# Two layers of a hybrid decoder on one core: six of eleven FFN chunks as Strassen pairs, rows normalised before the transposes, rope's addition on VectorE

## The chip, the core and the metric

One core of one Trainium2 chip runs the whole kernel as one program. The metric is the device time of one execution in microseconds (us). Engine names are those of the profile: PE is TensorE's matmul, PEld its weight load, DVE is VectorE, ACT ScalarE, POOL GpSimd, SP the engine that issues the loads. PE reads its operands from SBUF and writes to PSUM, here eight banks of 128 x 512 floats.

## What is computed

The input is 256 tokens of 1024 floats. Two layers follow each other, and each adds two things to the tokens: a mixer of three attention groups and a SwiGLU FFN with 2816 hidden columns.

```python
h = rms_norm(x, attn_norm_g[l])
proj = h @ w_in[l]
...
mix = jnp.concatenate([merge_heads(moba), merge_heads(diff), merge_heads(dsa)], axis=-1)
x = x + mix @ w_out[l]

h2 = rms_norm(x, ffn_norm_g[l])
x = x + (jax.nn.silu(h2 @ w_gate[l]) * (h2 @ w_up[l])) @ w_down[l]
```

Queries and keys of the groups are normalised by head and turned by rope; the DSA group keeps the 64 best keys of each query by an indexer's scores.

## The kernel before

**Tiles.** The 256 tokens are two token tiles (t0, t1) of 128. The 1024 input columns are eight contraction tiles (kt) of 128, in two halves (hf): 0 to 3 and 4 to 7. The FFN's 2816 columns are eleven chunks (fc) of 256; a gate and an up chunk lie side by side, so one matmul gives 256 columns of gate and 256 of up in one bank.

**Three matmuls for one.** All large products are made from float32 values that are split into a high and a low part (`mm3`, L440 to L451): high times high, high times low, low times high. So a weight is loaded as 128 x 2048 floats into one of three `raw` buffers, its high part `wh` is written by ACT (`high_thread`, L403) and its low part `wl` = raw - wh by DVE (`low_thread`, L411; L418), each in two pieces of 1024 columns. Such a unit stands in one of four HL slots until PE has used it (`drop`). The normalised tokens are split in the same way into `hH` and `hL` (L486), the mixers' output into `mH` and `mL`, the FFN's hidden values into `dqk_f4`.

**One layer.** The projection into eight groups of columns (`project`, L1143), the mixers, the output projection with w_out (L1264 to L1284), the norm of the result (`norm`, L512), and the FFN: chunk by chunk gate and up, 2 token tiles x 8 kt x 3 = 48 matmuls of 512 columns, and one chunk later down, 24 matmuls (L1312 to L1350).

**The norm.** When a token tile's half is added to the tokens (`residual_thread`, L528), PE transposes it at once (L465), DVE multiplies by the gain (L481), ACT writes the high part and DVE the low part (L486). The row's factor `rx` is made beside that: ACT squares (L496), POOL adds, scales and raises to the power -1/2 (L508, L455, L458). It is used only behind the matmuls, in `glu_thread` (L1003, L1007) and by the mixers.

**Rope.** DVE multiplies the bank by two tables (L549, L552, L561), POOL adds the two products (L570), and POOL also makes each head's factor (L455, L458, L605, L611). Keys are then multiplied by it on DVE (L658) and transposed by PE.

**What sets the order.** Threads yield operations to a planner (`Timeline`, L73), which keeps a clock for each engine, takes the operation that can start first (by rank where they tie) and writes each engine's instructions down in that order. Copies may go to ACT or DVE. So every engine runs a fixed list and stops at an instruction whose inputs aren't there. SP issues the loads in the order of `plan`, each when its `raw` buffer is free.

Of the kernel before, what the change touches and what calls it, by code (L numbers as in the profile page):

```python
# [15 lines left out]
P = 128  # L16
# [32 lines left out]

OUT_ORDER = [(0, 1), (6, 7), (2, 3), (4, 5)]  # L50


class Slots:


    def __init__(self, tiles):
        self.free = [(0.0, n, t) for n, t in enumerate(tiles)]
        self.index = {id(t): n for n, t in enumerate(tiles)}

# [113 lines left out]
def hybrid_block(  # L173
# [105 lines left out]
    PT = slots(8, [P, 3 * P], "pT")  # L279
# [3 lines left out]
    mT = tuple(tile_([P, KT, S], F32R, tag=f"m{e}") for e in "HL")  # L283
    mH, mL = mT
    rc = tile_([P, NT, 6, HD], tag="rc")
    rs = tile_([P, NT, 6, HD], tag="rs")
    iqT = tile_([P, 4, S], tag="iqT")
    ikT = tile_([P, 1, S], tag="ikT")
    sqT, skT = tile_([P, 2, S], tag="sqT"), tile_([P, 2, S], tag="skT")
    mqT, mkT = sqT, skT  # L290
    sv, mv = [[tile_([P, 256], tag="v") for t in range(NT)] for _ in range(2)]
    dv = [tile_([P, 512], tag="dv") for t in range(NT)]
    sco = [tile_([P, S], tag="sco") for t in range(NT)]
# [63 lines left out]
    plan = []  # L357
    for l in range(depth):
        for name in CHUNKS:
            c0, c1 = CHUNKS[name]  # L360
            for kts in chunk_units(l, name):
                plan.append(((l, name, kts[0]), load_cols(w_in[l], kts, c0, c1)))
        for kts in OUT_ORDER:
            plan.append(((l, "out", kts[0]), load_cols(w_out[l], kts, 0, D)))
        for fc in range(NFC + 1):
            if fc < NFC:
                for kts in (lo4, hi4):
                    plan.append(((l, "gu", fc, kts[0]), load_gu(l, fc, kts)))
            if fc > 0:
                plan.append(  # L370
                    ((l, "down", fc - 1), load_cols(w_down[l], [2 * fc - 2, 2 * fc - 1], 0, D))
                )
    units = {
        key: {"n": n, "w": w, "dma": dma, "raw": Event(),
              "h": [Event() for _ in range(0, n, PIECE)],
              "ready": [Event() for _ in range(0, n, PIECE)]}
        for key, (n, w, dma) in plan
    }
    ahead = [0]

    def load_thread():
        for n, u in enumerate(units.values()):
# [12 lines left out]
            raw = yield ("get", RAW)  # L395
            u["tile"] = raw
# [6 lines left out]
    def high_thread():  # L403
        for u in units.values():
            yield ("wait", u["raw"])
            u["hl"] = yield ("get", HL)
            for n, cs in enumerate(pieces(u["n"])):
                t = yield copy_op(u["hl"][0][:, cs], u["tile"][:, cs], cs.stop - cs.start, True)
                u["h"][n].done(t)

    def low_thread():  # L411
        for u in units.values():
            for n, cs in enumerate(pieces(u["n"])):
                yield ("wait", u["h"][n])
                (h, lo), raw = u["hl"], u["tile"]
# [5 lines left out]
            RAW.put(raw, t)  # L421
            ahead[0] += 1

    def split_rank():
        return 5 if ahead[0] < 2 else 60

# [42 lines left out]
    def norm_thread(t, hf, g0, ready):  # L469

        yield ("wait", x_ready[t][hf])
        bank = yield ("get", BANK)
        b = quarters(bank)
        yield transposes(
            [(b[:, j, :], xt[t][:, (4 * hf + j) * P : (4 * hf + j + 1) * P]) for j in range(4)]
        )
        xg = yield ("get", W2)
# [4 lines left out]
        BANK.put(bank, e)  # L482
        ks = slice(4 * hf, 4 * hf + 4)
# [3 lines left out]
        W2.put(xg, e)  # L487
        ready.done(e)

    def square_thread(t, hf, first, both):  # L490
        yield ("wait", x_ready[t][hf])
        yield ("wait", first)
# [19 lines left out]
    def norm(g0):  # L512
# [3 lines left out]
        for t in range(NT):  # L516
            both = Event(2)
            for hf in range(2):
                tl.spawn(norm_thread(t, hf, g0, h_ready[t][hf]), 0)
                tl.spawn(square_thread(t, hf, h_ready[t][hf], both), 1)  # L520
# [14 lines left out]
    def rope_apply(bank, b, nh, cv, sv_, dst):  # L535
# [34 lines left out]
        e = yield G(150 + 2.2 * n, lambda: nc.gpsimd.tensor_add(dst, dst, bb))  # L570
# [58 lines left out]
    def qk_thread(t, bank, full, r_ready, parts, rstd, done, r_done):  # L629
# [9 lines left out]
        read = yield from rope_apply(bank, b, 8, rc[:, t, js], rs[:, t, js], q)  # L639
# [27 lines left out]
    def idx_thread(t, bank, full, r_ready, done):  # L667
# [22 lines left out]
        yield from to_pairs(q, [iqT[:, 1:4, :], ikT], t, own)  # L690
# [3 lines left out]
    def sv_iq_thread(t, bank, full, r_ready, done, v_done):  # L694
# [6 lines left out]
        e = yield copy_op(sv[t], bank[:, 0:256], 256, scale=rx[t], bank=bank)  # L701
# [3 lines left out]
        yield from to_pairs(q[:, 0:2, :], [iqT[:, 0:1, :]], t, own)  # L705
# [11 lines left out]
    def indexer(t, ready, done, rank):  # L717
# [3 lines left out]
        sc = sco[t][:, :n]  # L721
# [3 lines left out]
        for g in range(4 // per):  # L725
# [3 lines left out]
            def scores():  # L729
                for i in range(per):  # L730
                    for e in range(2):
                        rows = slice(HD * e, HD * e + HD)
                        nc.tensor.matmul(
                            two[e][:, i * n : (i + 1) * n], iqT[rows, g * per + i, toks(t)],
# [116 lines left out]
    def get_pTs(n):  # L851
        got = []
        for _ in range(n):
            got.append((yield ("get", PT)))
# [15 lines left out]
    def plain_out(t, pTs, se, v, kt0, ready, used, done):  # L870
# [11 lines left out]
        if used.count == 0:  # L882
            for pT in pTs.values():
                PT.put(pT, used.time)
# [13 lines left out]
        h, lo = mH[:, ks, toks(t)], mL[:, ks, toks(t)]  # L898
# [47 lines left out]
    def diff_out(l, t, aTs, ready, used, done):  # L946
# [37 lines left out]
        h, lo = mH[:, 2:6, toks(t)], mL[:, 2:6, toks(t)]  # L984
# [433 lines left out]
```

## Time and profile before

| | us |
|---|---|
| median of 3 runs | 668.76 (668.53 to 668.90) |
| the profiled execution | 668.79 |
| its span, first to last instruction | 667.0 |
| PE busy, DVE busy, ACT busy, POOL busy | 650.0, 440.0, 357.1, 116.4 |
| FFN of layer 0, from the last residual of its norm on | 150.5 to 336.0 |
| FFN of layer 1 | 482.5 to 663.4 |

The page gives each engine's busy time, the span in 40 slices, the chain of work that ended last, and groups of instructions by line with the mean time of one. In a row of the timeline stand the start, the time taken, the engine, the line, the operation, out<-in with shapes, and in brackets the idle time before it with what ended it. A duration reaches to the instruction's end; the next may start earlier, so the distance from start to start is the cost in a row of equal ones.

### The profile page before, as it was taken

The numbers are of one execution on the slowest core, as the hardware profiler recorded it, in microseconds if no ns is written. First come the engines' busy times: TensorE is split into PE (matmuls) and PEld (weight loads), VectorE is DVE, ScalarE is ACT, GpSimd is POOL, SyncE is SP. The second block draws the span as 40 slices with busy tenths as digits, with TensorE's granted clock in tenths as the row PEclk, the third lists the DMA queues.
The fourth block names the chain that finished last, engine by engine and source line by source line (L and its number), as shares of the span: only waits on it lengthen the run. The fifth ranks groups of instructions, "written<-read, shape, count | busy, mean of one in ns | idle before, by whom it ended". The sixth has DMA issues, their size and how long they took to land.

```text
span 667.0 us, 8918 instructions
## 1 busy us (share of the span) xinstructions
PE 650.0 (97%) x3252; PEld 535.7 (80%) x3252; DVE 440.0 (66%) x782; ACT 357.1 (54%) x668; POOL 116.4 (17%) x143
## 2 busy tenths in 40 slices
PE   8899999999999999999999998999999999999997
PEld 7776778887888888888888777788878888888886
DVE  5789999568555555555486999964855555555542
ACT  5566759547444444444356585876554444444430
POOL 1818460104100000000022466401000000000000
PEclk9999999999999999999999999999999999999999
DMA  8982333535655555555447036343375556656501
GB/s 245 324 270 63 128 127 129 188 122 170 214 190 190 189 190 189 189 187 167 151 144 252 20 108 223 103 162 106 123 234 189 190 189 190 190 189 190 189 1 63
DMA packets 73775, 111.28 MB, mean 167 GB/s; under 512 B 2658, under 2 KB 54660, under 8 KB 73732
## 3 DMA queue, kind: packets, MB, share of 16 engines
q1 hardware_dynamic: 73700, 110.71, 51.4%
q8 instruction: 25, 0.41, 0.3%
q14 instruction: 18, 0.15, 0.1%
q10 hardware_dynamic: 32, 0.01, 0.0%
HBM read 109.66 MB, written 1.05 MB: 166 GB/s over the span
## 4 chain that ended last, share of the span: by engine, by line
PE 77%; DVE 13%; POOL 6%; DMA 2%; issue 1%; ACT 1%; SPq 0%; POOLq 0%; ACTq 0%
PE bank L447 23%; PE bank L449 23%; PE bank L448 23%; PE bank L465 4%; DVE wl L418 3%; PE bank L866 2%; POOL qr L570 2%; DVE sco L766 1%; DVE sco L755 1%; POOL rs L1129 1%; POOL rq L458 1%; DVE small L765 1%; PE bank L816 1%; DVE qr L549 1%; DVE small L596 1%
## 5 line engine op out<-in xcount | busy, mean ns | idle before, releaser
L418 DVE TENSOR_TENSOR wl<-raw,wh 128x1024 fp32r<-128x1024 f32 (+4 forms) x209 | 252.9, 1227 | 60.7 <-ACT wh L234 57.2
L234 ACT ACTIVATE wh<-raw 128x1024 fp32r<-128x1024 f32 (+3 forms) x208 | 211.2, 1039 | 68.6 <-PE bank L449 54.6
L447 PE MATMUL bank<-wh,hH 128*128 128x512 f32 (+3 forms) x608 | 238.9, 393 | 0.3 <-ACT hH L234 0.3
L449 PE MATMUL bank<-wh,hL 128*128 128x512 f32 (+3 forms) x608 | 231.8, 381 | 0.8 <-DVE hL L486 0.8
L448 PE MATMUL bank<-wl,hH 128*128 128x512 f32 (+3 forms) x608 | 231.5, 381 | 0.0
L447 PEld LDWEIGHTS bank<-wh,hH 128*128 128x128 f32 x608 | 114.4, 188 | 23.0 <-issue 3.6
L449 PEld LDWEIGHTS bank<-wh,hL 128*128 128x128 f32 x608 | 114.2, 188 | 22.9 <-DVE hL L486 1.6
L448 PEld LDWEIGHTS bank<-wl,hH 128*128 128x128 f32 x608 | 114.5, 188 | 18.5
L1003 ACT ACTIVATE p<-bank,rx 128x256 f32<-128x256 f32 x44 | 20.9, 475 | 121.0 <-PE bank L449 121.0
L1007 DVE SCALAR_TENSOR_TENSOR p<-bank,rx,p 128x256 f32<-128x256 f32 x44 | 21.3, 484 | 90.2 <-ACT p L1003 90.2
L447 PE MATMUL bank<-wh,dqk_f 128*128 128x512 f32 x176 | 70.2, 399 | 0.0
L449 PE MATMUL bank<-wh,dqk_f 128*128 128x512 f32 x176 | 68.8, 391 | 0.0
L448 PE MATMUL bank<-wl,dqk_f 128*128 128x512 f32 x176 | 68.7, 390 | 0.0
L508 POOL TENSOR_TENSOR ss<-ss 128x1 f32<-128x1 f32 x8 | 2.6, 328 | 240.6 <-ACT w L496 240.6
L234 ACT ACTIVATE dqk_f<-bank 128x256 fp32r<-128x256 f32 (+1 forms) x52 | 21.6, 415 | 32.7 <-PE bank L465 32.6
L449 PEld LDWEIGHTS bank<-wh,dqk_f 128*128 128x128 f32 x176 | 33.0, 188 | 7.0
L448 PEld LDWEIGHTS bank<-wl,dqk_f 128*128 128x128 f32 x176 | 33.1, 188 | 6.4
L447 PEld LDWEIGHTS bank<-wh,dqk_f 128*128 128x128 f32 x176 | 33.1, 188 | 6.3
L570 POOL TENSOR_TENSOR qr<-qr,w 128x512 f32<-128x512 f32 (+2 forms) x24 | 32.5, 1356 | 28.3 <-DVE w L561 13.8
L1019 DVE TENSOR_TENSOR dqk_f<-bank,dqk_f 128x256 fp32r<-128x256 f32 x44 | 18.5, 421 | 23.0 <-ACT dqk_f L234 23.0
L465 PE MATMUL bank<-ident,qr 128*128 128x128 f32 x116 | 20.9, 283 | 9.9 <-DVE qr L658 5.9
L797 ACT ACTIVATE p<-p,small 128x128 f32<-128x128 f32 (+1 forms) x64 | 28.5, 448 | 3.2 <-DVE small L786 3.2
(111 smaller groups left out, 658.1 us busy)
## 6 DMA issues: line engine op xcount, KB each, us to landing
raw<-in_w_in_dram SPq DMA_DIRECT2D x22, 1024.0 KB, 5.1
raw<-in_w_gate_dram SPq DMA_DIRECT2D x44, 512.0 KB, 3.9
raw<-in_w_up_dram SPq DMA_DIRECT2D x44, 512.0 KB, 5.1
raw<-in_w_down_dram SPq DMA_DIRECT2D x22, 1024.0 KB, 5.0
raw<-in_w_out_dram SPq DMA_DIRECT2D x8, 1024.0 KB, 4.9
raw<-in_w_in_dram SPq DMA_DIRECT2D x4, 768.0 KB, 6.3
raw<-in_w_in_dram SPq DMA_DIRECT2D x2, 912.0 KB, 5.0
raw<-in_w_in_dram SPq DMA_DIRECT2D x3, 456.0 KB, 4.9
```

The costliest lines, as they stand in the source:

```text
L234: nc.scalar.activation(dst, src, AF.Copy)
L418: lambda: nc.vector.tensor_sub(lo[:, cs], raw[:, cs], h[:, cs].bitcast(F32)),
L447: nc.tensor.matmul(o, aH[:, kt, tok], wH[:, k, cols], start=start, stop=False)
L448: nc.tensor.matmul(o, aH[:, kt, tok], wL[:, k, cols], start=False, stop=False)
L449: nc.tensor.matmul(o, aL[:, kt, tok], wH[:, k, cols], start=False, stop=stop)
L465: nc.tensor.transpose(o, i, ident)
L570: e = yield G(150 + 2.2 * n, lambda: nc.gpsimd.tensor_add(dst, dst, bb))
L797: lambda: nc.scalar.activation(p[:, spans[t]], p[:, spans[t]], AF.Exp, bias=mn[:, t : t + 1], scale=-1.0, accum_out=se[t],),
L866: nc.tensor.matmul(o, pT[:, toks(t)], v[0][:, cols], start=True, stop=t == 0)
L1003: FC, lambda: nc.scalar.activation(ff, bank[:, 0:FC], AF.Silu, scale=rx[t]), ap=1, bank=bank
L1007: lambda: nc.vector.scalar_tensor_tensor(ff, bank[:, FC : 2 * FC], rx[t], ff, op0=OP.mult, op1=OP.mult),
L1019: e = yield V(256, lambda: nc.vector.tensor_sub(lo, b2[:, 0:2, :], h.bitcast(F32)), bank=bank2)
```

## The change

**Strassen pairs.** Of the eleven chunks, (2, 3), (5, 6) and (8, 9) are computed in pairs. The normalised tokens are a 2 x 2 block matrix A (token tile by contraction half), the weights of the two chunks a 2 x 2 block matrix B (contraction half by chunk). Plain, that is eight block products of 12 matmuls; the pair takes seven: P1 = A11 B11, P7 = S3 T3, Q5 = S1 T1, P6 = S2 T2, Q3 = S4 B22, P2 = A12 B21, Q4 = A22 T4. The token sums S1 to S4 are made once a layer (`a_sums_thread`) by four additions or subtractions on DVE, and split like the tokens. The weight sums T1 to T4 of each pair are made on DVE by `sums_thread` from unsplit weights, 2048 columns each, into the buffers of weights that are no longer needed, and are split like weights: seven units a pair for four. ACT copies P1 and Q5 out of PSUM, and DVE combines the products in seven operations of 512 columns (`strassen_thread`) before silu and multiplication. Between Q3 and P2 stands the down product of the chunk before.

**Buffers.** The extra weights need three more buffers E a layer. They are the mixers' buffers, which now share memory with them: the rope tables and scores (`tb`), and `mH` and `mL` once the output projection is over. The token sums lie where the probabilities and values were (`pv`), the kept tokens and hidden values where queries and keys were (`qk`).

**Rows normalised first.** Sums over token tiles need normalised rows, so the FFN's norm now waits for `rx`, multiplies the row by it, and only then transposes.

**First token tile.** The output projection goes (0, 1) of t0, (0) of t1, (2, 3) of t0, (1) of t1, (2, 3) of t1, where it went (0, 1) of t0 and t1, (2, 3) of t0 and t1.

**Rope.** The addition is DVE's.

```diff
+BLOCKS = [(0,), (1,), (2, 3), (4,), (5, 6), (7,), (8, 9), (10,)]
...
+        def third(i, j):
+            b12, b22, t3 = loads[l, "gu", j, 0], loads[l, "gu", j, 4], units[l, "T3", i]
...
+            e = yield from add(t3, b12["held"].tile, b22["held"].tile)
...
+            yield from add(t1, b11["held"].tile, b12["held"].tile)
+            e = yield from add(t2, t3["held"].tile, b11["held"].tile, units[l, "gu", i, 0])
+            t3["held"].used(e)
+            if after:
+                yield from third(*after)
+            yield ("wait", b21["raw"])
+            e = yield from add(t4, t2["held"].tile, b21["held"].tile, t2)
...
-    def norm_thread(t, hf, g0, ready):
+    def norm_thread(t, hf, g0, ready, r_ready, kept):
...
+        if r_ready:
+            yield ("wait", r_ready)
+            src = yield ("get", W2)
+            yield copy_op(src, xt[t][:, cs], 512, True, scale=rx[t])
...
+        sums = (
+            (w2, a21, a22, True), (a21, a11, a21, True), (a11, w2, a11, True), (a12, a12, a11, False)
+        )
...
-        e = yield G(150 + 2.2 * n, lambda: nc.gpsimd.tensor_add(dst, dst, bb))
+        e = yield add_op(dst, dst, bb, n)
...
+            for us, t in (((0, 1), 0), ((0,), 1), ((2, 3), 0), ((1,), 1), ((2, 3), 1)):
...
+                steps = [
+                    ("P1", (lo8, 0), (l, "gu", i, 0)),
+                    ("P7", s3, (l, "T3", i)),
+                    ("Q5", s1, (l, "T1", i)),
+                    ("P6", s2, (l, "T2", i)),
+                    ("Q3", n4, (l, "gu", j, 4)),
+                    None,
+                    ("P2", (hi8, 0), (l, "gu", i, 4)),
+                    ("Q4", (hi8, 1), (l, "T4", i)),
+                ]
```

How the lists of the engines change is shown at three places. Lines are those of each kernel; the numbers are buffers. First DVE at the start of layer 0's FFN. Before:

```order
L528 TENSOR_TENSOR x_1_71<-x_1_71,bank1_64 128x512
L418 TENSOR_TENSOR wl_25_100<-raw_17_92,wh_24_99 128x1024
L481 TENSOR_TENSOR w2_27_102<-bank3_66,gcol_6_80 128x512
L528 TENSOR_TENSOR x_1_71<-x_1_71,bank5_68 128x512
L418 TENSOR_TENSOR wl_25_100<-raw_17_92,wh_24_99 128x1024
L486 TENSOR_TENSOR hL_73_148<-w2_27_102,hH_72_147 128x4x128
```

Now, from the second half's residual of t0 on to the first silu product:

```order
L698 TENSOR_TENSOR x_1_71<-x_1_71,bank3_66 128x512
L248 TENSOR_SCALAR w2_27_102<-x_1_71,rx_69_144 128x512
L494 TENSOR_TENSOR wl_25_100<-raw_17_92,wh_24_99 128x1024
L612 TENSOR_TENSOR qk_91_1362<-bank7_70,gcol_6_80 128x512
L612 TENSOR_TENSOR qk_91_1362<-bank0_63,gcol_6_80 128x512
L698 TENSOR_TENSOR x_2_72<-x_2_72,bank2_65 128x512
L619 TENSOR_TENSOR hL_65_140<-qk_91_1362,hH_64_139 128x4x128 x2
L494 TENSOR_TENSOR wl_25_100<-raw_17_92,wh_24_99 128x1024
L698 TENSOR_TENSOR x_2_72<-x_2_72,bank4_67 128x512
L612 TENSOR_TENSOR qk_91_1362<-bank5_68,gcol_6_80 128x512
L503 TENSOR_TENSOR mL_93_1396<-tb_90_1343,mH_92_1395 128x1024
```

Before, a gain (L481) follows its residual at once; now both halves of t0 are added before the first gain (L612), a weight split stands ahead of the last residual, and the first weight sum (L503) inside the norm.

Second, DVE between a later pair's product P6 and its combinations, where before a chunk looked like this:

```order
L418 TENSOR_TENSOR wl_23_98<-raw_15_90,wh_22_97 128x1024 x2
L1007 SCALAR_TENSOR_TENSOR p_33_108<-bank0_63,rx_92_167,p_33_108 128x256
L1019 TENSOR_TENSOR dqk_f4_109_1407<-bank7_70,dqk_f4_109_1407 128x2x128
L418 TENSOR_TENSOR wl_25_100<-raw_16_91,wh_24_99 128x1024 x2
L1007 SCALAR_TENSOR_TENSOR p_38_113<-bank6_69,rx_93_168,p_38_113 128x256
```

```order
L1201 TENSOR_TENSOR w2_28_103<-bank0_63,w2_29_104 128x512
L503 TENSOR_TENSOR raw_17_92<-raw_17_92,raw_16_91 128x1024
L494 TENSOR_TENSOR wl_21_96<-raw_16_91,wh_20_95 128x1024
L503 TENSOR_TENSOR raw_17_92<-raw_17_92,raw_16_91 128x1024
L494 TENSOR_TENSOR wl_21_96<-raw_16_91,wh_20_95 128x1024
L503 TENSOR_TENSOR qr_31_106<-qr_30_105,w2_28_103 128x512
L494 TENSOR_TENSOR wl_23_98<-raw_17_92,wh_22_97 128x1024
L1201 TENSOR_TENSOR w2_28_103<-bank7_70,w2_28_103 128x512
```

The sum T4 (L503), the splits of P2's and Q4's weights (L494) and the combinations (L1201) alternate on one list, and the combination that waits for P6 stands first.

Third, SP's loads around the second pair. Before, and now:

```order
L338 DMA raw_16_91<-in_w_gate_dram 128x4x256
L338 DMA raw_16_91<-in_w_up_dram 128x4x256
L325 DMA raw_17_92<-in_w_down_dram 128x2x1024
L338 DMA raw_15_90<-in_w_gate_dram 128x4x256
L338 DMA raw_15_90<-in_w_up_dram 128x4x256
```

```order
L338 DMA raw_15_90<-in_w_down_dram 128x2x1024
L351 DMA raw_16_91<-in_w_gate_dram 128x4x256
L351 DMA raw_16_91<-in_w_up_dram 128x4x256
L351 DMA mH_92_1395<-in_w_gate_dram 128x4x256
L351 DMA mH_92_1395<-in_w_up_dram 128x4x256
L351 DMA mL_93_1396<-in_w_gate_dram 128x4x256
L351 DMA mL_93_1396<-in_w_up_dram 128x4x256
L351 DMA raw_15_90<-in_w_gate_dram 128x4x256
```

The loads of the next pair's second chunk into the extra buffers (mH, mL) stand ahead of the single chunk's first load (raw_15) on the one queue.

More of the change, by code (lines that the diff above doesn't have):

```diff
@@ L355, in chunk_units, with __init__, used, unit @@
         return [lo4, hi4]
-    plan = []
+    loads = {}
+    sequence = []
+    units = {}
+    class Held:
+        def __init__(self, uses):
+            self.uses, self.when, self.tile, self.slots = uses, 0.0, None, None
+        def used(self, when):
+            self.uses -= 1
+            self.when = max(self.when, when)
+            if self.uses == 0:
+                self.slots.put(self.tile, self.when)
+    def unit(key, n, w, held, raw):
+        count = len(range(0, n, PIECE))
+        units[key] = {
+            "n": n, "w": w, "held": held, "raw": raw if raw else [Event() for _ in range(count)],
+            "h": [Event() for _ in range(count)], "ready": [Event() for _ in range(count)],
+        }
@@ L361, in hybrid_block @@
             for kts in chunk_units(l, name):
-                plan.append(((l, name, kts[0]), load_cols(w_in[l], kts, c0, c1)))
+                load((l, name, kts[0]), load_cols(w_in[l], kts, c0, c1))
         for kts in OUT_ORDER:
[L364 to L378, printed above, removed]
+            load((l, "out", kts[0]), load_cols(w_out[l], kts, 0, D))
+        plan_ffn(l)
     ahead = [0]
     def load_thread():
-        for n, u in enumerate(units.values()):
+        for n, u in enumerate(loads[key] for key in sequence):
             if n in X_FIRST:
@@ L638, in qk_thread @@
         js = slice(parts[0][2], parts[-1][2] + 1, 3)
-        read = yield from rope_apply(bank, b, 8, rc[:, t, js], rs[:, t, js], q)
+        read = yield from rope_apply(bank, b, 8, cur["rc"][:, t, js], cur["rs"][:, t, js], q)
         yield ("wait", ev["read"])
@@ L1288, in main, with f4_of, get @@
+            for tag in ("mH", "mL"):
+                E[l].add(tile_([P, 2048], tag=tag, own=False), e)
+            f4s = []
+            def f4_of(fc):
+                def get():
+                    yield ("wait", kept["over"])
+                    if not f4s:
+                        f4s.append(tile_([P, 4, 4, S], F32R, tag="qk", own=False))
+                    return f4s[0][:, fc % 4]
+                return get
             fev = [[Event() for t in range(NT)] for fc in range(NFC)]
@@ L1352, in hybrid_block @@
+            yield from down_block(before)
     lam_ready = Event()
```

406 lines of the change are left out of this document (301 added, 105 removed).

## Prediction

> **What bounds the kernel now.** I read the page from its top: busy time, then the slices, then the chain that ended last.
>
> ```profile
> PE 650.0 (97%) x3252; PEld 535.7 (80%) x3252; DVE 440.0 (66%) x782; ACT 357.1 (54%) x668; POOL 116.4 (17%) x143
> PE   8899999999999999999999998999999999999997
> DVE  5789999568555555555486999964855555555542
> POOL 1818460104100000000022466401000000000000
> PEclk9999999999999999999999999999999999999999
> PE 77%; DVE 13%; POOL 6%; DMA 2%; issue 1%; ACT 1%; SPq 0%; POOLq 0%; ACTq 0%
> ```
>
> PE (TensorE) is busy for 97% of the span at full clock, and the chain runs over it for 77%. DVE (VectorE) has two faces: nines in both mixers (the 4th to 7th slice and the 23rd to 26th), fives in both FFNs. The windows give both stages in numbers:
>
> ```profile
> 16.70:100.00 83.30, 77.06 (x427) 62.43 (x428) 77.16 (x186) 52.79 (x112) 48.99 (x54) 1.00 0.55 182
> 150.50:336.00 185.50, 185.12 (x838) 151.78 (x837) 103.87 (x118) 87.79 (x119) 9.92 (x15) 1.00 0.57 183
> 482.50:663.40 180.90, 180.44 (x814) 147.54 (x812) 92.22 (x108) 77.75 (x105) 0.94 (x3) 1.00 0.51 166
> ```
>
> After the span, PE, PEld, DVE, ACT and POOL stand in that order. In the FFN of layer 0 (second row) PE works 185.1 of 185.5 us and DVE 103.9: only fewer matmuls can shorten this stage, and DVE has 81.6 us to give. In the first mixer DVE is busy for 77.16 of 83.3 us; there PE idles 6.2 us, and the waits name what for:
>
> ```profile
> PE bank L465 <- DVE qr L658: 5.9, 9, 1.0
> PE bank L465 <- POOL qr L570: 1.9, 3, 0.9
> PE bank L465 <- DVE qr L686: 1.5, 1, 1.5
> ```
>
> They are transposes that wait for the last step of a key, of an index row or of rope: 9.3 us over both layers.
>
> **Removed: 72 matmuls.** A Strassen pair takes 7 products of 12 matmuls where two plain chunks take 96 matmuls, so a pair saves 12, and six pairs 72.
>
> ```profile
> 240.08 0.39 PE L447 MATMUL bank<-wh,hH 128*128 128x512 f32 x1
> ...
> 240.76 0.39 PE L447 MATMUL bank<-wh,hH 128*128 128x512 f32 x1
> ...
> 336.82 1.91 PE L465 MATMUL bank<-ident,x 128*128 128x128 f32 x16
> ```
>
> The rows last 0.39 us because they overlap; what counts is start to start, (240.76 - 240.08) / 3 = 0.227 us. 72 x 0.227 = **-16.3 us**, all of it on the path, since PE never waits there. A transpose costs 1.91 / 16 = 0.12 us; their number stays the same.
>
> **Added: work on VectorE.** Its price is start to start too when it works without a pause:
>
> ```profile
> 451.62 2.36 DVE L418 TENSOR_TENSOR wl<-raw,wh 128x1024 fp32r<-128x1024 f32 x2 [2.22 <-ACT wh L234]
> 147.33 0.69 DVE L528 TENSOR_TENSOR x<-x,bank 128x512 f32<-128x512 f32 x1 [0.19 <-PE bank L449]
> 337.63 1.88 DVE L481 TENSOR_TENSOR w<-bank,gcol 128x512 f32<-128x512 f32 x3
> 445.92 0.42 DVE L889 TENSOR_TENSOR qr<-bank,se 128x256 f32<-128x256 f32 x1
> 446.26 0.17 DVE L886 RECIPROCAL se<-se 128x4 f32<-128x4 f32 x1
> 471.01 1.22 DVE L418 TENSOR_TENSOR wl<-raw,wh 128x1024 fp32r<-128x1024 f32 x1
> 478.03 1.22 DVE L418 TENSOR_TENSOR wl<-raw,wh 128x1024 fp32r<-128x1024 f32 x1
> ```
>
> One 1024-column operation lasts 1.22 us, two in a row 2.36, so the pitch is 1.14. By the same reading 512 columns cost 0.60 ((1.88 - 0.69) / 2, with 0.69 for one alone), and 256 cost 0.34 (446.26 - 445.92). A pair adds three weight units to split (6 x 1.14), four weight sums (8 x 1.14) and seven combinations of 512 columns: 16.0 + 4.2 = 20.2 us. Three pairs and the eight 512-column operations that form the token sums (4.8) make 65.4 us a layer: of the 81.6 us of slack, 81.6 - 65.4 - 8.2 = 8.0 are left in a stage that is 8.2 us shorter. DVE goes to some 95%.
>
> So the average fits, barely; what matters is each stretch, since only four split units (HL) can stand ready.
>
> *A later pair.* From one pair to the next PE does 204 matmuls (48 of a single chunk, 84 of a pair, 72 of three down products) and 12 transposes: 46.3 + 1.4 = 47.7 us. By the order, DVE does 32 operations of 1024 columns, 7 of 512 and 12 of 256 in it: 36.5 + 4.2 + 4.1 = 44.8 us, 94%. In its tightest part, from product P6 to the second weights of the next single chunk, I lay DVE's rows end to end (the first combination can start when P6 ends; 8.2 us later PE wants P2's weights, 10.9 later Q4's, 13.6 later the next chunk's): P2's are split after 0.6 + 4 x 1.14 = 5.2, Q4's after 8.7, the chunk's first after 12.2. Everything is ready 1.4 to 3 us early. I take 0.3 us of waiting for each of four such pairs, **+1** (0 to 4).
>
> *The first pair of a layer* has less lead, because the token sums and the first weight sums stand in front of it. From the second token tile of chunk 0 to the second weights of chunk 4, PE does 216 matmuls and 8 transposes, 49.9 us; DVE does 34, 14 and 7 operations, 38.8 + 8.4 + 2.4 = 49.6, and begins about 3.5 us later (its last split of the norm is wanted after 12 matmuls and two more, 3.2, and a 0.34 stands behind it). The last half unit is wanted 6 matmuls (1.4 us) later: 3.5 + 49.6 - 49.9 - 1.4 = 1.8 late. I take 1.5 for each layer, **+3** (0 to 9).
>
> [...]
>
> ACT gets the same six splits a pair and two copies:
>
> ```profile
> L234 ACT ACTIVATE wh<-raw 128x1024 fp32r<-128x1024 f32 x197 | 203.4, 1055 | 65.5 <-PE bank L449 54.6 <-DMA raw<-in_w_in_dram 7.1 <-issue 1.7
> L234 ACT ACTIVATE dqk_f<-bank 128x256 fp32r<-128x256 f32 x44 | 16.8, 382 | 24.2 <-PE bank L465 24.1
> ```
>
> 18 x 1.06 = 19 us and some 9 us of smaller copies on 87.8 of 185.5: hidden, at nothing, as long as its queue isn't blocked by a product that it waits for. Four transposed results and a chunk's result must share four free banks at a pair's end: one eviction (ACT 0.38, DVE 0.34) may show once a layer, **+1** (0 to 2).
>
> **Rows normalised first.** The transposes now wait for the row's factor, so POOL's steps stand between residual and matmul:
>
> ```profile
> 147.71 0.61 ACT L496 ACTIVATE w<-x 128x512 f32<-128x512 f32 x1
> 148.24 0.18 ACT L496 ACTIVATION_READ_ACCUMULATOR w<-x 128x1 f32 x1
> 148.50 0.19 POOL L508 TENSOR_TENSOR ss<-ss 128x1 f32<-128x1 f32 x1 [18.23 <-ACT w L496]
> 148.78 0.19 POOL L455 TENSOR_SCALAR rx<-ss 128x1 f32<-128x1 f32 x1
> 149.06 0.55 POOL L458 TENSOR_TENSOR rx<-rx,nhalf 128x1 f32<-128x1 f32 x1
> L591 ACT ACTIVATE w<-bank,rx 128x512 f32<-128x512 f32 x14 | 9.6, 687 | 10.2 <-PE bank L449 5.6 <-DVE w L552 1.7 <-issue 1.6
> ```
>
> Residual 0.69 (its row stands above), square and read 0.8, POOL 1.1 (148.50 to 149.61), scaling 0.69, transposes 0.5, gain 0.69, high part 0.6, low part 0.69: 5.8 us with hand-overs of about 0.1 each 6.4. For the first token tile the new order leaves 36 matmuls (8.2 us) behind it, where 24 (5.4) stood: covered. For the second, chunk 0 of the first tile covers 24 matmuls and 8 transposes, 6.4. In DVE's and ACT's queues a weight split (1.14, 1.06) stands ahead at one place each. I take 0.5 a layer, **+1** (0 to 6).
>
> **Rope's addition moves** from POOL to DVE, 24 times.
>
> ```profile
> L570 POOL TENSOR_TENSOR qr<-qr,w 128x512 f32<-128x512 f32 x16 | 22.5, 1405 | 15.0 <-DVE w L552 11.1 <-DVE w L561 3.9
> 22.52 2.28 DVE L418 TENSOR_TENSOR wl<-raw,wh 128x1024 fp32r<-128x1024 f32 x1
> 22.56 1.15 POOL L570 TENSOR_TENSOR qr<-qr,w 128x448 f32<-128x448 f32 x1
> ```
>
> 1.4 us and two hand-overs become 0.60 on an engine that is there already, and POOL's power steps no longer queue behind it. DVE gains some 6 us of work a layer where it is 93% busy, but such an addition can hold up a DVE operation beside it (2.28 instead of 1.22). Both ends: the 9.3 us of waits go but for a third (-6), or half of DVE's 12.5 us (16 x 0.60 and 8 shorter) shows on PE (+6). The keys' factor on POOL stays on the path, so I take a quarter of the waits, **-2.5**.
>
> Table building for layer 1 (POOL) now waits for the buffer tb; it has the last 120 matmuls (27 us) as cover: 0. The load bytes are the same.
>
> **Sum**, against the profiled execution's 668.79 us (span 667.0, 1.8 around it; the median 668.76 is the same): -16.3 + 1 + 3 + 1 + 1 - 2.5 = -12.8, so **656.0 us**.
>
> **Rivals.**
> *VectorE binds in the FFN (slower than before)*: if alternating sums, splits and combinations cost 1.22, 0.69 and 0.42 each, start to start, the first stretch takes 54.1 us of DVE, so it is 1.8 + 4.5 = 6.3 late, and a later period 49.0 where PE needs 47.7, with no room for a wait, some 2 late. 2 x 6.3 + 4 x 2 = 20.6 stand where the sum has 4: 672.5. It decides from a pitch of about 1.21 (47.7 of 44.8 times 1.14) on. For it: DVE at 95%, with no stage of this length to compare with. Against: the 2.36 for two, and the 1.88 for three. 7%. [...]
> *Loads starve the pairs (slower)*: SP issues in order, and a pair's two loads into the extra buffers now stand ahead of the next chunk's raw loads. If such a buffer comes free late, all behind it are late by a landing:
>
> ```profile
> raw<-in_w_gate_dram SPq DMA_DIRECT2D x44, 512.0 KB, 3.9
> raw<-in_w_up_dram SPq DMA_DIRECT2D x44, 512.0 KB, 5.1
> ```
>
> 5.1 us at each of six pairs is 31 us, less some 10 that the split units ready ahead give: 677. It decides where an extra buffer frees less than 5.1 us before the sum that reads it. In my laying-out it frees some 10 us before. 4%.
> *The mixers get longer*: DVE has 6.1 us free in the 83.3 of the first mixer's window and gets 6 more; if half of its 12.5 us over both layers shows on PE, +6 stands where the sum has -2.5: 664.5. 7%.
> *The waits go and DVE keeps ahead*: rope -6, and +2 where the sum has +6 for pairs, norms and banks: 648.5 to 651. 15%.
> *It doesn't do what it says*: PE's order holds 3014 rows' instructions for 3086, so the 72 are gone; 3% that something else takes up their time, 669.
>
> **Numbers.** The forecast's own band, 651 to 662, has 64%. The range, 649.5 to 664.5, takes in the rivals on the mixers and on the waits; the rest, 14%, is left out. A measurement of this kernel tells about 0.2% (1.3 us) from no change. Faster: 64 + 15 + 7 = 86%; same, the last rival and a little of the forecast's edge, 4%; slower, the two slower rivals with their nearer misses, 10%.
>
> **What would show it.** PE: 72 matmuls fewer, pitch still 0.227, clock 1.00; FFN windows 5 to 8 us shorter with DVE near 95%. PE's waits in the FFN should name DVE wl, mostly in the first pair of each layer, under 2 us each. Waits for qr in the mixers shrink. I am wrong if PE waits for raw loads, if DVE's pitch in the pairs is 1.22, or if the mixers are longer than before.

## The result, and the profile after

The changed kernel takes 656.68, 658.17 and 660.56 us in three executions; a fourth, 790.24 us at a granted clock of 0.752, was disturbed and is left out of the comparison, but stands in the stated median of 659.37. Before ran 668.64 beside it. The ratio is 0.985, 95% interval 0.9812 to 0.9888. Run again for the experiments (e9), after took 655.67 to 658.38, median 657.19, ratio 0.9821 (0.9805 to 0.9837). The forecast was 656.0.

The profiled execution took 656.68 us, its span 654.9: 12.1 us less than before's 667.0. The page of after, busy times first, then slices and the chain:

```profile
PE 636.6 (97%) x3180; PEld 522.6 (80%) x3180; DVE 560.0 (86%) x948; ACT 403.5 (62%) x746; POOL 89.4 (14%) x119
...
PE   9999999989999999999999999999999999999997
...
DVE  5889999557999989999578899995499998999961
...
POOL 1507430010000000080020315301100000000000
PEclk9999999989999999999999999999999999999999
...
PE 63%; DVE 25%; DMA 4%; issue 3%; POOL 2%; ACT 2%; SPq 0%; DVEq 0%; ACTq 0%; POOLq 0%
```

PE has 72 instructions fewer. DVE's fives in both FFNs have become nines, and its share of the chain has gone from 13 to 25%. PE's row and the clock's have an 8 in the ninth slice, which was not forecast.

I cut the span where a stage's wide matmuls begin or end. The rows of after at the six cuts (first matmul, end of the output projection, end of the FFN, and the same for layer 1):

```profile
8.59 0.45 PE L569 MATMUL bank<-wh,hH 128*128 128x456 f32 x1
...
151.35 0.39 PE L571 MATMUL bank<-wh,mL 128*128 128x512 f32 x1
...
333.44 0.40 PE L571 MATMUL bank<-wh,qk 128*128 128x512 f32 x1
...
335.88 0.48 PE L569 MATMUL bank<-wh,hH 128*128 128x456 f32 x1 [0.30 <-ACT hH L240]
...
468.70 0.39 PE L571 MATMUL bank<-wh,mL 128*128 128x512 f32 x1
...
650.82 0.39 PE L571 MATMUL bank<-wh,qk 128*128 128x512 f32 x1
```

Before's six starts are 8.43, 150.11, 336.59, 339.03, 476.39 and 662.93. So mixer and output projection together went from 141.7 to 142.8 us in layer 0 (**+1.1**) and from 137.4 to 132.8 in layer 1 (**-4.5**), the FFNs from 186.5 to 182.1 (**-4.4** each). With 0.16 more ahead of the first matmul that is the 12.1. The same edit shortened one mixer and lengthened the other, and each FFN got little more than half of the 8.2 us that its 36 matmuls are worth.

The windows of after for the first mixer, the FFN of layer 0 and its first 78 us:

```profile
16.70:100.00 83.30, 80.89 (x454) 66.65 (x454) 76.24 (x186) 55.15 (x116) 35.32 (x43) 1.00 0.55 184
151.60:333.40 181.80, 179.10 (x808) 145.88 (x807) 164.94 (x192) 109.05 (x148) 16.89 (x15) 1.00 0.61 199
156.30:234.60 78.30, 75.84 (x342) 61.24 (x341) 77.50 (x91) 50.07 (x67) 0.00 (x0) 1.00 0.66 216
```

In the mixer PE works 80.89 us of 83.3 where it worked 77.06, with DVE no busier (76.24; 77.16 before). In the FFN DVE is busy 91%, below the forecast's 95, but the mean hides what the last row shows: for 78 us it pauses 0.8 us in all.

What PE waits for in after (us, times, longest), the FFN's and the mixers' mixed:

```profile
PE bank L571 <- DVE hL L619: 2.5, 4, 1.1
...
PE bank L587 <- DVE qk L1189: 1.9, 2, 1.0
...
PE bank L587 <- DVE qr L828: 1.7, 3, 0.7
...
PE bank L569 <- ACT mH L242: 1.2, 1, 1.2
...
PE bank L587 <- DVE p L1177: 1.2, 2, 0.6
...
PE bank L571 <- DVE qk L1189: 1.0, 2, 0.5
...
PE bank L587 <- DVE qr L1146: 0.9, 1, 0.9
...
PE bank L571 <- DVE mL L1158: 0.6, 1, 0.6
```

Three things are to be seen. The mixers' waits for qr (9.3 us before) have shrunk to the 1.7 of L828. A split weight (`wl`) is not among the releasers: in this execution PE never stands idle for one. (In e9's, of the same kernel, it does, for 1.1 us.) Instead it waits for results on their way through DVE: a chunk's silu product and hidden values (`p` L1177, `qk` L1189) and the norm's low part (`hL`). And the three waits at L1146, L242 and L1158, 2.7 us together, lie in one place, the end of layer 0's output projection.

### The profile page after: what moved, and what is told of

It reads as the page before. It is cut to its first block, busy times and chain, and to the rows that moved or that the text cites. A ratio compares the mean times of both kernels' runs of the same rounds, so it can differ in the third digit from the quotient of the medians.

```text
span 654.9 us, 8906 instructions
## 1 busy us (share of the span) xinstructions
PE 636.6 (97%) x3180; PEld 522.6 (80%) x3180; DVE 560.0 (86%) x948; ACT 403.5 (62%) x746; POOL 89.4 (14%) x119
## 4 chain that ended last, share of the span: by engine, by line
PE 63%; DVE 25%; DMA 4%; issue 3%; POOL 2%; ACT 2%; SPq 0%; DVEq 0%; ACTq 0%; POOLq 0%
PE bank L571 18%; PE bank L569 18%; PE bank L570 18%; DVE wl L494 10%; PE bank L587 4%; DMA mH<-in_w_up_dram 2%; PE bank L1036 1%; DVE raw L503 1%; DVE qr L503 1%; PE bank L986 1%; DMA raw<-in_w_in_dram 1%; ACT wh L240 1%; DMA w<-in_diff_lambda_dram 1%; DVE w L1201 1%; POOL rq L580 1%
## 5 line engine op out<-in xcount | busy, mean ns | idle before, releaser
L494 DVE TENSOR_TENSOR wl<-raw,wh 128x1024 fp32r<-128x1024 f32 (+4 forms) x209 | 250.0, 1204 | 16.1 <-ACT wh L240 15.4
L240 ACT ACTIVATE wh<-raw 128x1024 fp32r<-128x1024 f32 (+4 forms) x208 | 210.1, 1039 | 84.8 <-PE bank L571 34.8
L569 PE MATMUL bank<-wh,hH 128*128 128x512 f32 (+3 forms) x488 | 191.8, 393 | 0.3 <-ACT hH L240 0.3
L571 PE MATMUL bank<-wh,hL 128*128 128x512 f32 (+3 forms) x488 | 185.5, 380 | 2.5 <-DVE hL L619 2.5
L570 PE MATMUL bank<-wl,hH 128*128 128x512 f32 (+3 forms) x488 | 184.8, 379 | 0.0
L571 PE MATMUL bank<-wh,qk 128*128 128x512 f32 x176 | 68.8, 391 | 1.0 <-DVE qk L1189 1.0
L569 PE MATMUL bank<-wh,qk 128*128 128x512 f32 x176 | 69.4, 394 | 0.0
L570 PE MATMUL bank<-wl,qk 128*128 128x512 f32 x176 | 68.6, 390 | 0.0
L571 PEld LDWEIGHTS bank<-wh,qk 128*128 128x128 f32 x176 | 33.0, 188 | 8.7 <-DVE qk L1189 1.9
L570 PEld LDWEIGHTS bank<-wl,qk 128*128 128x128 f32 x176 | 33.1, 188 | 6.5
L569 PEld LDWEIGHTS bank<-wh,qk 128*128 128x128 f32 x176 | 33.0, 188 | 6.5
L569 PE MATMUL bank<-wh,pv 128*128 128x512 f32 x96 | 37.3, 389 | 0.0
L570 PE MATMUL bank<-wl,pv 128*128 128x512 f32 x96 | 37.3, 389 | 0.0
L571 PE MATMUL bank<-wh,pv 128*128 128x512 f32 x96 | 37.3, 389 | 0.0
```

The lines of the kernel that those rows point to most:

```text
L240: nc.scalar.activation(dst, src, AF.Copy)
L494: lambda: nc.vector.tensor_sub(lo[:, cs], raw[:, cs], h[:, cs].bitcast(F32)),
L569: nc.tensor.matmul(o, aH[:, kt, tok], wH[:, k, cols], start=start, stop=False)
L570: nc.tensor.matmul(o, aH[:, kt, tok], wL[:, k, cols], start=False, stop=False)
L571: nc.tensor.matmul(o, aL[:, kt, tok], wH[:, k, cols], start=False, stop=stop)
```

## Experiments

All were timed in five rounds, each ratio against the runs of the kernel before on the same chip (medians 669.1 to 669.6). The stages are cut as above, on each profiled execution; us throughout. PE's wide matmuls stand one to three lines lower in e6, e7 and e12; e5 has the lines of before. Where an operation is added or removed, the planner also moves others: in e6, for instance, some fifty of PE's 3180 instructions stand at another place than in after.

| kernel | median | ratio to before (95%) | mixer 0 | FFN 0 | mixer 1 | FFN 1 | span |
|---|---|---|---|---|---|---|---|
| before | 668.64 | 1 | 141.7 | 186.5 | 137.4 | 186.5 | 667.0 |
| after | 659.37 | 0.985 (0.9812-0.9888) | 142.8 | 182.1 | 132.8 | 182.1 | 654.9 |
| e9 after again | 657.19 | 0.9821 (0.9805-0.9837) | 142.3 | 183.1 | 132.8 | 182.0 | 655.1 |
| e4 no pairs | 669.27 | 1.0002 (0.9988-1.0016) | 142.8 | 188.8 | 132.8 | 188.3 | 667.8 |
| e5 rope alone | 662.33 | 0.9896 (0.9880-0.9912) | 139.6 | 186.5 | 133.3 | 186.5 | 660.9 |
| e3 rope on POOL | 660.85 | 0.9870 (0.9848-0.9893) | 142.9 | 182.1 | 136.9 | 182.4 | 659.6 |
| e2 old order | 652.25 | 0.9751 (0.9733-0.9769) | 138.2 | 181.0 | 131.9 | 184.3 | 650.2 |
| e1 wait filled | 656.88 | 0.9813 (0.9794-0.9831) | 141.4 | 183.3 | 132.8 | 182.9 | 655.8 |
| e6 sum twice | 670.56 | 1.0019 (1.0007-1.0031) | 142.8 | 188.9 | 132.8 | 188.7 | 668.6 |
| e7 sum thrice | 686.34 | 1.0254 (1.0232-1.0276) | 142.9 | 196.8 | 133.2 | 196.4 | 684.6 |
| e8 late pairs | 654.71 | 0.9798 (0.9773-0.9822) | 142.0 | 181.7 | 132.8 | 180.7 | 652.5 |
| e10 old order, late pairs | 652.86 | 0.9766 (0.9745-0.9787) | 138.1 | 183.3 | 131.9 | 182.8 | 650.8 |
| e11 order by layer, late pairs | 652.58 | 0.9755 (0.9740-0.9771) | 138.2 | 183.2 | 132.8 | 180.8 | 650.4 |
| e12 both by layer | 650.55 | 0.9733 (0.9710-0.9756) | 138.1 | 180.1 | 132.8 | 180.7 | 646.8 |

**What the pairs are worth (e4).** All else stays as in after.

```diff
-BLOCKS = [(0,), (1,), (2, 3), (4,), (5, 6), (7,), (8, 9), (10,)]
+BLOCKS = [(n,) for n in range(11)]
...
-            tl.spawn(a_sums_thread(kept, s_ready), 3)
+            kept["over"] = kept["split"]
...
-                    tl.spawn(sums_thread(l), sums_rank)
```

> All eleven chunks alone, and no token sums; rows normalised first, rope on VectorE and the new order of the output projection stay. 72 matmuls come back. Theory A (the 4 us of waits that each FFN has gained belong to the pairs): the FFN stages last 186.3 us as before, 4.4 more than after, and the time is 8.8 us above after, 665.5. Rival (the waits belong to the rows that are normalised first, or to the smaller pool of banks): FFN stages of 188 to 190 us, 669 to 673, no better than before.

The rival's numbers came: FFNs of 188.8 and 188.3 us, and a total no better than before. The FFNs are 6.7 and 6.2 us longer than in after, so the pairs gain 12.9 of their 16.3 us; the other 3.4 are what their own waits cost beyond the waits that only e4 has. But theory A was wrong that all waits belong to the pairs: without them the FFNs are 2.3 and 1.8 us longer than before, so rows normalised first have a price of their own. The waits for `p` and `qk` do belong to the pairs; e4 has none. Without the pairs the rest of the change brings nothing (1.0002). PE's rows of e4 where the second token tile of chunk 0 begins, ACT's ahead of them:

```profile
157.64 1.28 ACT L1174 ACT_TABLE_LOAD   x1
...
159.21 0.62 ACT L240 ACTIVATE hH<-qk 128x512 fp32r<-128x512 f32 x1
...
159.89 0.50 PE L569 MATMUL bank<-wh,hH 128*128 128x512 f32 x1 [1.74 <-ACT hH L240]
```

The norm's high part waits in ACT's queue behind chunk 0's silu, whose table load alone takes 1.28 us. In after the planner put that silu behind the high part; there the low part waits in DVE's queue behind a weight sum, 0.41 us in layer 0 and 1.06 in layer 1, where the sum itself waits 0.75 us for its load.

**What rope's move is worth (e5 and e3).** In e5 the kernel before gets this one edit; in e3 after gets it undone.

```diff
-        e = yield G(150 + 2.2 * n, lambda: nc.gpsimd.tensor_add(dst, dst, bb))
+        e = yield V(n, lambda: nc.vector.tensor_tensor(dst, dst, bb, op=OP.add))
```

> The kernel before, with rope's addition on VectorE as the only edit. Theory A (the move is worth 3.5 to 4.5 us a mixer; the rest of the change, without pairs, gives it back in the first output projection and at the start of each FFN): mixers of 137 to 138.5 and 133 to 133.5 us where before has 141.7 and 137.4, FFN stages unchanged at 186.5, 660 to 662 in all. Rival (the move helps only together with the outputs that are waited for by token tile): under 3 us better than before, 666 to 669.

> Rope's addition is back on POOL (24 times), the rest as after. Theory A (the shorter mixers come from this move): the window from 16.7 to 100 us has 3 to 4 us less PE work in it, waits for qr are back near 9 us, and the time is 6 to 9 us more than after, 663 to 666. Rival (the mixers became shorter because each token tile's output no longer waits for the other's): under 2 us more, 657 to 659.

Alone it takes 2.1 us from the first mixer and 4.1 from the second, 6.1 in the span. Theory A holds in the second mixer and a little less in the first, where 139.6 misses the stated 137 to 138.5; the time, 662.33, is just above its 660 to 662. The first mixer's window in e3, to be read against after's row above:

```profile
16.70:100.00 83.30, 74.90 (x408) 60.42 (x409) 75.27 (x180) 50.64 (x102) 47.24 (x53) 1.00 0.53 182
```

And what PE waits for there:

```profile
PE bank L587 <- DVE qr L828: 7.4, 9, 1.7
...
PE bank L587 <- POOL qr L740: 2.2, 3, 1.2
...
PE bank L587 <- DVE qr L856: 1.7, 2, 1.2
```

PE does 74.90 us of work in it where after does 80.89, and the waits for qr are back at 11.3 us: the move is what shortened them. Yet over the whole stage, undoing it costs 4.1 us in layer 1 and only 0.2 in layer 0, so the total is below theory A's band: in layer 0 the gain had already been given back. There e3 lacks the three waits at the end of layer 0's output projection (from 127 to 140 us PE is busy all the time) and the half clock that follows them in after.

**Where layer 0 gives it back (e2).** The rows of after, at the end of the output projection's first token tile:

```profile
131.29 0.69 DVE L1146 TENSOR_TENSOR qr<-bank,small 128x512 f32<-128x512 f32 x1 [6.56 <-POOL small L580]
...
132.04 0.66 PE L587 MATMUL bank<-ident,qr 128*128 128x128 f32 x4 [0.88 <-DVE qr L1146]
...
133.90 0.50 PE L569 MATMUL bank<-wh,mH 128*128 128x512 f32 x1 [1.21 <-ACT mH L242]
...
135.24 0.50 PE L571 MATMUL bank<-wh,mL 128*128 128x512 f32 x1 [0.61 <-DVE mL L1158]
...
138.22 0.63 PE L571 MATMUL bank<-wh,mL 128*128 128x512 f32 x1
...
139.08 0.63 PE L570 MATMUL bank<-wl,mH 128*128 128x512 f32 x1
```

The last mixer result of the first tile passes through DVE, PE, ACT and DVE again, and PE has nothing else to do: the change moved 12 matmuls of the second tile behind this point, to cover the norm. The last two rows show the sequel: they are two matmuls apart, 0.43 us for each from start to start where 0.227 is usual: half clock (granted share 0.50 from 136.2 to 139.6 us). e2 puts the 12 back:

```diff
-            for us, t in (((0, 1), 0), ((0,), 1), ((2, 3), 0), ((1,), 1), ((2, 3), 1)):
+            for us, t in (((0, 1), 0), ((0, 1), 1), ((2, 3), 0), ((2, 3), 1)):
...
-                if us == (1,):
+                if us == (0, 1) and t == 1:
```

> The output projection in the order of the kernel before (units 0 and 1 of both token tiles, then units 2 and 3 of the first tile, then of the second); the rest as after. Theory A (layer 0's wait is there because 12 matmuls of the second tile were put behind the first tile's last): the 2.7 us of waits between 131 and 136 us go, with them the 1.7 us of half clock, and the second layer, which had no such wait, loses up to 2 us where the norm's chain has 5.4 us of cover and not 8.2: 652.5 to 655.5 in all. Rival (the early end of the first tile is worth its place: the norm's chain of 6.4 us shows in both layers): 657 to 660. Rival (the wait is late data, whatever the order): as after, 656.7.

Theory A holds, and the time is slightly below its band. The window from 128 to 136 us in after and in e2, each with that view's columns as above:

```profile
128.00:136.00 8.00, 5.30 (x35) 4.07 (x34) 4.07 (x5) 4.76 (x19) 2.62 (x4) 1.00 0.01 3
```

```profile
128.00:136.00 8.00, 8.00 (x51) 6.80 (x50) 2.72 (x4) 4.54 (x20) 2.43 (x4) 1.00 0.01 3
```

The 2.7 us are gone, and mixer 0 is 4.6 us shorter (2.7 and the 1.7 of half clock make 4.4). The new order alone doesn't make the wait: e3 has it too, and there the planner put 12 wide matmuls ahead of the first transposes of that result, where after's layer 0 has 3. Layer 1 pays: its FFN is 2.2 longer, 1.7 of it another half-clock stretch (granted clock 0.997 over the span, an 8 in the 29th slice of the clock's row), its mixer 1.0 shorter.

**Whether the half clock follows from the wait (e1, e9).** In e1 PE transposes the identity while it waits, for nobody:

```diff
-        e = yield transposes([(b2[:, h, :], onv[:, h, :]) for h in range(4)])
+        fill = l == 0 and t == 0
...
+        def turn():
+            for n in range(7 * fill):
+                nc.tensor.transpose(b2[:, n % 4, :], ident, ident)
+            for h in range(4):
+                nc.tensor.transpose(b2[:, h, :], onv[:, h, :], ident)
+            for n in range(10 * fill):
+                nc.tensor.transpose(b[:, n % 4, :], ident, ident)
...
+        e = yield T(436, turn)
```

> Layer 0 only: in the wait at the end of the mixer PE does 17 transposes of the identity that nobody reads (7 ahead of the four real ones of the first token tile, 10 behind them); nothing else moves. Theory A (the half-speed stretch of 3.4 us follows from PE's idling 3.1 us in the 5.3 us ahead of it): the granted clock is 1.00 throughout, the matmuls at 136 to 140 us are 0.227 apart again, and the span is about 1.7 us shorter than the 654.9 of the kernel after, 653.2. Theory B (the dip comes by itself, whatever PE does): clock 0.997 as before and 654.9. Theory C (the added transposes delay the real ones): clock 1.00 but the span no shorter, 654.5 to 656.

> The kernel after, unchanged, beside the two below on one chip. Theory A (a stretch of 3.4 us at half clock, 1.7 us each, is what its own times differ by): most executions show clock 0.997, 656.5 to 659. Rival (the spread has another cause): the clock and the time go apart.

The windows of e1 (two rows), and of e9, which has after's wait unfilled:

```profile
128.00:136.00 8.00, 7.15 (x53) 6.02 (x52) 3.84 (x5) 4.76 (x19) 2.62 (x4) 1.00 0.01 3
136.00:140.00 4.00, 3.99 (x20) 3.03 (x20) 1.98 (x3) 1.21 (x2) 0.00 (x0) 1.00 0.00 0
```

```profile
128.00:136.00 8.00, 5.30 (x36) 4.07 (x35) 3.78 (x4) 4.75 (x19) 2.28 (x4) 1.00 0.01 3
136.00:140.00 4.00, 4.00 (x19) 3.05 (x20) 2.05 (x3) 0.76 (x2) 0.34 (x1) 1.00 0.00 0
```

Filled, four of four executions have a clock of 0.999 or 1.0. Unfilled, three of e9's five have 0.997 (657.19, 658.25, 658.38) and two 0.999 or 1.0 (655.67, 656.89): the means differ by 1.7 us. So clock and time go together, as e9's theory A says. Only the profiled executions show where a dip lies, and there it follows the same wait in after and not in e9. The counts are small, and a dip comes without the wait too: before, which lacks it, shows 0.997 in 5 of the 52 executions timed beside the experiments. The other half of e1's theory A fell: the span is not shorter, 655.8, which is the number of theory C but not its reason, for the mixer is shorter. Its mixer gained 1.4 us, and its FFNs lost 1.2 and 0.8, in waits of 1.32 us at the first pair's end (0.93 in after) and for split weights. The FFN of e9's profiled execution, without a dip too, lost 1.1 in layer 0, most of it where chunk 1 waits for split weights. Its first such row:

```profile
165.50 0.50 PE L570 MATMUL bank<-wl,hH 128*128 128x512 f32 x1 [0.31 <-DVE wl L494]
```

What the dip costs in the end stays open: by e9's means 1.7 us, by the profiled executions nothing (654.9 with it, 655.1 without), but e9's also waits for split weights in the first mixer, at 24 to 26 us (0.8 us), where after doesn't. That time won ahead of the FFN is lost in it points at VectorE.

**Whether VectorE binds (e6, e7).** The third weight sum of each pair is written two or three times; no other line is changed.

```diff
             e = yield from add(t3, b12["held"].tile, b22["held"].tile)
+            e = yield from add(t3, b12["held"].tile, b22["held"].tile)
```

> After, with the third weight sum of each pair written twice: 2 x 1.14 = 2.3 us more work for VectorE in each pair, 13.7 in all, and nothing else. Theory A (VectorE has 2.9 us to spare from one pair to the next): 0 to 2 us above after, 657 to 660. Rival (VectorE binds there already, and every added us shows): 13.7 more, 670.

> After, with that sum written three times: 4.6 us more of VectorE in each pair, 27.4 in all. Theory A (2.9 us to spare in a later pair, none in the first): 1.7 us shows in each of four later pairs and up to 4.6 in each first one, 7 to 16 above after, 664 to 673. Rival (VectorE binds): 27 more, 684. Rival (VectorE is far from binding): as after, 657 to 659.

Theory A, which was the prediction's, falls twice. 13.7 us more work make the span 13.7 us longer (668.6 for 654.9; by e9's median 13.4), with the same single half-clock stretch as in after (clock 0.997 in both). All of it shows. 27.4 make it 29.7, but there the clock is 0.98, about eight stretches of 3.41 us at half clock where after has one (an estimate: 2 x 0.02 x 684.6 / 3.41), so e7's number isn't VectorE's alone. PE's waits in e6:

```profile
PE bank L571 <- DVE wl L494: 4.2, 8, 0.9
...
PE bank L588 <- DVE qk L1190: 2.7, 4, 0.7
```

Matmul by matmul against after, layer 0 of e6 loses 2.9 us ahead of the first pair, 2.2 at its end and 1.7 at the end of the second, and nothing at the third. (The third sum of a pair is made during the pair before, so none is added in the last.) And yet after shows no wait for `wl`. The rows of its tightest place, in chunk 1 of layer 1, the split, the weight load ahead of the matmul that reads it, and that matmul; then split and matmul at two later places:

```profile
485.32 1.21 DVE L494 TENSOR_TENSOR wl<-raw,wh 128x1024 fp32r<-128x1024 f32 x1
...
486.59 0.19 PEld L570 LDWEIGHTS bank<-wl,hH 128*128 128x128 f32 x1 [0.19 <-DVE wl L494]
...
486.66 0.43 PE L570 MATMUL bank<-wl,hH 128*128 128x512 f32 x1
...
528.14 1.21 DVE L494 TENSOR_TENSOR wl<-raw,wh 128x1024 fp32r<-128x1024 f32 x1
...
528.52 0.39 PE L570 MATMUL bank<-wl,hH 128*128 128x512 f32 x1
...
529.88 0.39 PE L570 MATMUL bank<-wl,hH 128*128 128x512 f32 x1
...
574.14 1.21 DVE L494 TENSOR_TENSOR wl<-raw,wh 128x1024 fp32r<-128x1024 f32 x1
...
577.56 0.39 PE L570 MATMUL bank<-wl,hH 128*128 128x512 f32 x1
```

The first is ready at 486.53 and read at 486.66: 0.13 us early, and even that isn't slack, for the weight load (PEld) already waits 0.19 us for the split; the matmul ahead, which runs from 486.44 to 486.83, hides it. Behind the first pair (528.14) it is 0.53 us, 529.35 to 529.88. Behind the second (574.14) it is 2.2, 575.35 to 577.56. The two engines arrive almost together, so no wait shows, and whatever is added to DVE ahead of that place does. In a layer's first 78 us VectorE is the bound as much as TensorE.

**Pairs one place later (e8), and what adds up (e10 to e12).**

```diff
-BLOCKS = [(0,), (1,), (2, 3), (4,), (5, 6), (7,), (8, 9), (10,)]
+BLOCKS = [(0,), (1,), (2,), (3, 4), (5,), (6, 7), (8,), (9, 10)]
```

> After, with each pair one place later: chunks 0, 1, 2 alone, then 3 and 4, 5 alone, 6 and 7, 8 alone, 9 and 10 last. The matmuls are the same number. Theory A (the first pair waits because token sums and weight sums stand ahead of it with too little lead): the waits of 0.6, 0.5 and 0.9 us ahead of and at the end of the first pair go, 1 to 2 us a layer, and the last pair's end is covered by the down products of chunk 8: 653 to 657. Rival (the last pair's combinations and four results stand bare at the layer's end): 3 to 4 us more a layer, 663 to 665.

> The output projection in the order of the kernel before, and each pair one place later; the rest as after. Theory A (the two losses are independent: 4.6 us at the end of the first output projection, 1 to 2 us in the two FFNs): 649 to 651.5. Rival (time won ahead of the FFN comes back as waits there, as with the filled wait, because VectorE works without a pause in its first stretch): no better than the order alone, 652 to 654.

> Pairs one place later, the output projection of the first layer in the order of the kernel before, that of the second layer in the order of after, which showed no wait there. Theory A (each layer has its better order): 0 to 2 us below the kernel with the old order in both layers, 648 to 650.5. Rival (the start of the second FFN costs the same either way): the same within 1 us.

> Layer 0 with the pairs where after has them and the old order of the output projection, layer 1 with the pairs one place later and the order of after: of each layer the arrangement that measured shortest (138.2 and 181.0; 132.8 and 180.8 us). Theory A (the stages add up): 2.5 us below the kernel with the old order alone in both layers, 649 to 651. Rival (what one stage wins, the next one waits): 652 to 653 again.

e8 supports theory A, in layer 0 with less than its 1 to 2 us: the FFNs are 0.4 and 1.4 us shorter than after's, the waits at the first pair gone, a new one of 1.74 at the FFN's start come (silu ahead of the norm, as in e4). e10 and e11 combine it with the old order and gain nothing over e2: FFN 0 is 183.3 and 183.2 where e2 had 181.0, with waits in e10 for `hL` (0.40 and 0.93) and a scaled row (0.37) at its start, so the rival holds there. e12 takes for each layer the pairs and the order that measured shortest, and here the stages add up in the profiled execution. The median, 650.55 us, is 1.7 below e2's, inside theory A's band, the best of all and 1% under after's. Its five executions run from 648.54 to 652.83, so its lead over e2 (651.93 to 653.80) is small beside the spread, and the intervals of the two ratios overlap.

## Why the prediction was right, and where it wasn't

The sum gave -12.8, the span gave -12.1 (the ratio 0.985 gives -10.0, e9's 0.9821 gives -12.0). Its largest term was right; the others were mis-sized in both directions and largely cancelled, so that the total came so close is luck.

*The matmuls, -16.3.* Right: the pitch is 0.227 still ((529.88 - 528.52) / 6, two `wl` matmuls six apart in the rows above), and e4 shows 12.9 net, 3.4 less, where the sum had +5 for pairs and banks.

*VectorE's pitch.* Right. Two rows of after, in a pair:

```profile
184.54 2.35 DVE L494 TENSOR_TENSOR wl<-tb,wh 128x1024 fp32r<-128x1024 f32 x2
186.81 2.35 DVE L494 TENSOR_TENSOR wl<-raw,wh 128x1024 fp32r<-128x1024 f32 x2
```

(186.81 - 184.54) / 2 = 1.14. So the rival at 1.22 does not hold in this stage either.

*Waits for split weights, +4 (first pairs +3, later pairs +1).* Measured none in after, and some 1 us, start to start, in layer 0 of e9's profiled execution. In after the weights came 0.13 us early in chunk 1 and 0.53 behind the first pair, not 1.8 late. The step that failed is the conclusion drawn from it: "Everything is ready 1.4 to 3 us early" reads as slack. For weights it was there (2.2 us behind the second pair), but of e6's 2.3 us 1.7 showed there too, 0.8 of it ahead of the chunk's results (`qk` L1190): they queue on VectorE at the same place, and my margin counted splits alone.

*Banks at a pair's end, +1.* The mechanism was right, the size double: the two waits for `qk` ahead of a transpose, 1.9 us together, lie at the end of each first pair. A wait in this view begins when the last transpose's 0.28 us are over; from its start to the next one's start it is 1.20 and 1.25 us, where transposes otherwise stand 0.11 apart.

*Rows normalised first, +1.* "In DVE's and ACT's queues a weight split stands ahead at one place each" had the right kind of cause and too small a size: 4.1 us without pairs (e4), in after 0.41 and 1.06 for `hL`. The same step failed worse at its other end. It counted which matmuls now stand behind the first tile ("leaves 36 matmuls (8.2 us) behind it, where 24 (5.4) stood: covered") and not that 12 were taken from in front of it, where they covered the mixer's last result. That is 4.6 us in layer 0 (e2), the largest loss that the sum lacked. In layer 1 the planner left 15 wide matmuls ahead of that result's transposes, and nothing waits; in after's layer 0 it left 3. Why it chose so differently stays open.

*A wait the sum didn't have.* The results of the first two chunks (`p` L1177, `qk` L1189 ahead of a matmul) stand in DVE's queue behind splits and weight sums: 1.2 + 1.0 us.

*Rope's addition, -2.5.* Mis-sized: -6.1 alone (e5), the end of the stated range. "The keys' factor on POOL stays on the path" fits the 1.7 us that are left of 9.3 (the keys' multiplication, L828, waits 3.6 us for POOL's factors in after); I had left three quarters.

*What would show it.* The pitch, the 72 matmuls and the shrinking waits for qr came as stated. The clock is 0.997 and not 1.00, the FFNs are 4.4 and not 5 to 8 us shorter, DVE stands at 91% of the first one's time and not 95, no wait of after names `wl`, and "if the mixers are longer than before" came true in layer 0.

Together: the mixers, but for the end of layer 0, are 8.0 us shorter (3.5 by e2, and 4.5) where the sum had 2.5; the FFNs gave back 7.6 of their 16.4 where it had 6; and 4.6 at the end of layer 0 it lacked. -5.5 + 1.6 + 4.6 is the 0.7 by which it missed. Of the 8.0, rope's move alone explains 6.1 (e5); where the other 1.9 come from was not looked into. The forecast's case came true in its total; by e6 the rival "VectorE binds" was closer to it than its 7% said, through the margin and not through the pitch.

## What to carry to other kernels

A profile without waits for an engine does not show that the engine has slack (here weights came 0.13 us early, and 13.7 us of added work made the span 13.7 us longer): measure from the end of its last result to its use, or double one of its operations and see how much of it shows. When work is moved to cover one chain, look at which chain it covered where it stood. And edits that each save time in a stage need not add up when another engine arrives 0.1 us ahead of the first.

## What the runs showed of the hardware

PE's clock fell to half for 3.4 us after three idle stretches of 0.88, 1.21 and 0.61 us within 4.1 us. The window of after:

```profile
136.00:140.00 4.00, 4.00 (x14) 2.99 (x13) 1.18 (x3) 0.69 (x1) 0.00 (x0) 0.57 0.00 0
```

The granted share is 0.5 from 136.2 to 139.6 and 1 on both sides; it comes as one stretch of 3.41 us or, in e7, where waits of 3.6 us stand at one place, two of them in a row:

```profile
169.30:176.10 6.80, 5.35 (x13) 4.19 (x14) 6.80 (x11) 1.28 (x3) 0.00 (x0) 0.50 0.60 171
```

It does not come every time: a clock of 0.997 or less shows in three of e9's five executions and in nine of e4's twelve, which has the same wait.

The clock records of after's trace hold, from 6.46 us on, stretches of 129.706, 3.413 and 515.413 us at one granted share each: 38.00, 1 and 151.02 times the shortest. Before's has one of 662.186 us, 194.02 times that. So I read the waits in stretches of 3.41 us. In after the one ahead of the half clock holds two of the three waits (1.21 us, all but its first 0.06, and 0.61); PE is busy in it for 1.65 us. In e9's profiled execution the same wait is 1.2 us long, and the granted clock is 1.00 before and after it. The two rows below meet at 133.93 us, within the wait; that an edge lies there is an estimate in steps of 3.413 us, for with full clock on both sides no record shows one. After's stretch, then e9's two:

```profile
132.75:136.16 3.41, 1.65 (x6) 0.97 (x6) 2.89 (x4) 1.36 (x4) 1.39 (x2) 1.00 0.02 5
```

```profile
130.52:133.93 3.41, 1.96 (x13) 1.25 (x11) 1.85 (x2) 2.76 (x10) 1.23 (x2) 1.00 0.03 7
133.93:137.35 3.42, 2.17 (x8) 1.20 (x9) 2.62 (x4) 0.84 (x4) 1.39 (x2) 1.00 0.00 0
```

That is one pair of executions, and nearly the same busy time comes without a dip: in e12 PE is busy for 1.67 us from 467.14 to 470.55 us, and no half clock follows (clock 1.00 in that execution). What decides was not shown.
